# An output projection in 2x2 blocks with seven products, and a feed-forward begun by six chunks on half the tokens

## The chip, the core and the metric

The kernel runs on one core of one Trainium2 chip. The metric is the device time of one execution in microseconds (us), lower being better. TensorE (PE in the profile) multiplies matrices, VectorE (DVE), ScalarE (ACT) and GpSimd (POOL) work elementwise, and SyncE (SP) starts most transfers. Transfers that SP starts run on one queue of DMA engines, those that POOL starts on another. A line such as L158 is line 158 of the kernel profiled.

## The reference

One layer of a decoder on 512 tokens of width 1024, in float32: a feed-forward, token mixing (a recurrent branch and a sliding-window attention side by side, merged by two sigmoid gates and projected by `w_out`), and a second feed-forward, each between two normalisations with learned gains. Cut to the part around the change:

```python
    merged = jax.nn.sigmoid(g_lru) * (y_lru @ w_proj_lru) + jax.nn.sigmoid(g_attn) * (y_attn @ w_proj_attn)
    return merged @ w_out
...
        h = h + rms_norm(m, mix_post_g[l])
        f = swiglu(rms_norm(h, ffn2_pre_g[l]), ffn2_w_gu[l], ffn2_w_down[l])
        h = h + MACARON_SCALE * rms_norm(f, ffn2_post_g[l])
```

## The kernel before

**Products.** Every large product is three matmuls (`mm3`, L157 to L160): each float32 operand is split in a rounded high part and a low part, and high by high, high by low and low by high are summed in PSUM. A weight tile of 128x1024 comes by a transfer on SP's queue (`wload`, L102), ACT rounds it (L112), and DVE subtracts to get the low part (L120). `wget` prepares two tiles ahead.

**Seven products for eight.** Most of both feed-forwards already runs with seven products of blocks in place of eight (`paired`, tiles `f2X`, `f2Y`, `f2Q`). The sums of weight blocks for their second matrix are made in DRAM: SP copies a block (L393), and POOL starts a transfer that accumulates another one onto it (L395).

**The mixer.** Eight gate chunks (`gate_chunk`, L1024) run beside the first heads of the attention. The rotary queries are combined on POOL (L936, L937; tiles `q0m`, `q1m`), stored to DRAM (`q_halves`, L960) and loaded back in another layout (`qt`, L965, four transfers) before the scores (L981, tiles `at00b`, `at10b`, ...). The softmax ends with a multiplication on POOL (L998), and transposes on PE follow (L1004). A loop over eight chunks (L1108 to L1117) then makes the second gated projection and the merged features: `mgh` (ACT, times 0.5, L1115) and `mgl` (DVE, L1116).

**The output projection.** `token_out` (L449) multiplies eight chunks of features by the eight weight tiles of `w_out`, for four tiles of 128 tokens and two halves of the columns: 64 blocks (tiles `woo`), 192 matmuls of 128x512. With `TAILS = 7` the last seven chunks are taken tile by tile, so the first tile of tokens is complete after 0.34 of the work. Behind each tile runs its `epilogue` from `boundary` (L482): squares (L502), an inverse root on POOL (L203), gain and residual (L506, L529), squares again (L534), a spill of the residual to DRAM (L537), the next gain (L542), and then `to_features` (L212): eight transposes on PE (tiles `b2ntp`), a cast to the high part (`u3h`, L222, ACT), the low part (`u3l`, L223, DVE) and a raw copy (`u3r`, L227, ACT), from which `moving` (L694) later makes the operands for `paired`.

**The start of the second feed-forward.** `first_four` (L238) takes four weight chunks with the first half of the tokens (tiles `f2f`, matmuls of 128x256), and then with the second half, so that it can start when two tiles of tokens are there. Four further chunks (tiles `f2g`) take all tokens at once.

**Order.** Except in a few stretches marked `manual_schedule`, a planner sets the order of each engine's instructions: it simulates the program and places each instruction by its own times. Each engine runs its list in order.

Of the kernel before, what the change touches and what calls it, by code (L numbers as in the profile page):

```python
# [42 lines left out]
def hybrid_block_kernel(ctx, tc, x, xt, g1, w_first, gains, gu1, gs1, dn1, w_x, w_gate, w_q, w_k, w_v, w_gl, w_ga, w_pl, w_pa,  # L43
# [70 lines left out]

    def wsplit(upto):
        while len(wready) < min(upto, wcap[0]):
            n = len(wready)
            wround(n + 1)
            w = whi[n]
            V.tensor_tensor(out=w[:, 1, :], in0=raws[n], in1=w[:, 0, :].bitcast(F32),  # L120
                            op=ALU.subtract)
# [3 lines left out]
    def wget():  # L125
        i = wpos[0]
        wpos[0] += 1
        wsplit(i + 1 + AHEAD)
        return wready[i]

# [107 lines left out]
    def first_four(u, name, done):  # L238
# [14 lines left out]
    def gate_up(u, name, first, fast, then, rs=None):  # L253
        ps = []
# [25 lines left out]

        first(u, f"{name}f", done)
        run = paired(fast, name, slot, then(ps))
        for j in range(2, JSTD[name]):
            if j == JSTD[name] - 1:
                next(run)
            bb = []
# [12 lines left out]
    def paired(fast, name, slot, then):  # L299
# [79 lines left out]
        for k in range(3):  # L379
            load(k)  # L380
        sums(0)
        parts(0, 1)
# [65 lines left out]

    def token_out(chunk, n, finish, name, tail_n):  # L449
        half, epilogue, _ = finish  # L450
        banks = {}

        def block(t, c, w, i):
            ph, pl = chunks[c]
            ts_ = slice(t * P, (t + 1) * P)
            if (t, i) not in banks:
                banks[t, i] = bank(f"{name}o{t}{i}")
            ns = slice(i * 512, (i + 1) * 512)
            mm3(banks[t, i], ph[:, c % 4, ts_], pl[:, c % 4, ts_], w[0][:, ns], w[1][:, ns], c == 0, c == n - 1)

        chunks = {}
        tail = []
        for c in range(n):
            w = wget()
            chunks[c] = chunk(c)
            if c < n - tail_n:
                for t in range(NT):
                    for i in range(2):
                        block(t, c, w, i)
                tick()  # L470
            else:
                tail.append((c, w))
        for t in range(NT):
            for i in range(2):
                for c, w in tail:
                    block(t, c, w, i)
            for i in range(2):
                half(t, i, banks[t, i])
            start(epilogue(t))
            tick()  # L480

    def boundary(src, dst, g_post, g_pre, u, scale, name, raw=None, then=None):  # L482
        rhs = []
# [10 lines left out]

        def half(t, i, z, sign=1.0, o=None):
            if t not in sq:
                sq[t], parts[t] = sm(f"{name}ps{t}", 2), [None, None]
# [4 lines left out]
            A.activation(t4(f"{name}sq{t}{i}")[:, :512], z, AF.Square, scale=1.0 / 32.0, accum_out=sq[t][:, i:i + 1])  # L502
            parts[t][i] = o

            def gain():
                V.scalar_tensor_tensor(out=o, in0=z, scalar=sign * scale, in1=g_post[:, cols[i]], op0=ALU.mult,  # L506
                                       op1=ALU.mult)

            if i == 0:
                gain()  # L510
            else:
                late[t] = gain

# [5 lines left out]
        def epilogue(t):  # L519
# [3 lines left out]
            r = inverse(sq[t], f"p{t}")  # L523
            late[t]()
            yield
# [247 lines left out]

    def first_unscaled(u, name, done):
        bs = [bank(f"{name}{i}") for i in range(4)]
# [316 lines left out]
    for c in range(KD):  # L1092
# [12 lines left out]
    while live:  # L1105
        tick()
    mg = []
    for c in range(KD):  # L1108
        s, b = sig_gate(c, ya, "ga")
        if c % 4 == 0:  # L1110
            mg.append((b8(f"mgh{c}", [P, 4, T], F32R), b8(f"mgl{c}", [P, 4, T], F32R)))
        V.scalar_tensor_tensor(out=s, in0=s, scalar=1.0, in1=b, op0=ALU.add, op1=ALU.mult)
        V.tensor_tensor(out=s, in0=s, in1=m1[c // 4][:, c % 4, :], op=ALU.add)
# [6 lines left out]
    u3 = new_u("u3")  # L1120
    hs2 = [dram.tile([P, D], F32, name=f"h2_spill{t}") for t in range(NT)]
    raw3 = [b8(f"u3r{i}", [P, 4, T]) for i in range(2)]
    mv3 = {}
    finish = boundary(hs, hs2, g_post, g_pre, u3, 1.0, "b2", raw3, lambda: moving(raw3, "u3", mv3))
    for _ in range(2):
        finish[2]()
# [11 lines left out]
def _layout(inputs):  # L1138
# [47 lines left out]
    a["w_pa"] = chunks(wa)  # L1186
    a["w_o"] = c(f["w_out"].reshape(KD, P, D))
    a["gu2"], a["gs2"] = gu(f["ffn2_w_gu"])[:JSTD["f2"]], pairs_of(f["ffn2_w_gu"], JSTD["f2"])
# [40 lines left out]
```

## Time and profile before

| what | value |
|---|---|
| median of 3 runs | 1119.62 us (1118.8 to 1120.09) |
| the profiled execution | 1119.82 us |
| its span | 1118.0 us |
| PE busy | 1103.2 us, 6558 matmuls |
| DVE busy | 895.0 us |
| ACT busy | 591.8 us |
| POOL busy | 78.0 us |
| first matmul of the output projection | 728.90 us |
| first matmul of the paired stage of the second feed-forward | 823.03 us |

The span is the profiled stretch from its first to its last instruction; the 1.82 us between it and the time of the same execution lie around it. In a timeline a row gives the start, the length, the engine, the line and the tiles, and in brackets how long the engine stood idle before and what released it. Matmuls overlap in the pipeline, so a matmul's cost is the distance between starts rather than its length.

### The profile page before, as it was taken

To read this page: it belongs to the slowest core of one execution; us is meant where nothing else is said; L and a number is where in the kernel's file an instruction comes from. 1 tells how busy PE (TensorE), PEld (TensorE's weight loads), DVE (VectorE), ACT (ScalarE), POOL (GpSimd) and SP (SyncE) were. 2 spreads that over 40 slices of the span, in tenths; PEclk is the share of its full clock that TensorE was granted. 3 is DMA by queue.
4 is the path that set the end of the run, shared out by engine and by line. 5 is a ranking of instruction groups with operands and counts; after the bars stand their busy time and mean duration, and the time that the engine had idled before them with its cause. 6 is when DMAs were issued, how large, how long until landed. Compare 5 with 4: busy or idle time off the path is not lost.

```text
span 1118.0 us, 16771 instructions
## 1 busy us (share of the span) xinstructions
PE 1103.2 (99%) x6558; PEld 982.3 (88%) x6558; DVE 895.0 (80%) x1277; ACT 591.8 (53%) x991; POOL 78.0 (7%) x82
## 2 busy tenths in 40 slices
PE   9999999999999999999999999999999999999997
PEld 7889999988878888788888888888999999998885
DVE  6998898889998788999777462546859888988895
ACT  7445555465664757576555351436435455556561
POOL 1000000000000101123112000001000000000000
PEclk9999999999999999999999999999999999999999
DMA  9239999664677173622812340523348999455473
GB/s 364 77 125 256 314 280 299 196 226 130 222 266 260 55 207 113 170 57 76 263 58 95 113 169 19 207 95 132 113 122 255 299 274 310 117 173 192 146 269 115
DMA packets 53280, 202.07 MB, mean 181 GB/s; under 512 B 6353, under 2 KB 6481, under 8 KB 48465
## 3 DMA queue, kind: packets, MB, share of 16 engines
q1 hardware_dynamic: 45424, 163.77, 43.3%
q0 software_dynamic: 3456, 23.07, 10.6%
q10 hardware_dynamic: 4320, 14.16, 3.4%
q8 instruction: 51, 0.84, 0.3%
q14 instruction: 29, 0.23, 0.1%
HBM read 189.44 MB, written 57.67 MB: 221 GB/s over the span
## 4 chain that ended last, share of the span: by engine, by line
PE 88%; DVE 8%; issue 1%; DMA 1%; ACT 1%; POOL 0%; SPq 0%; DVEq 0%; POOLq 0%; ACTq 0%
PE f2X L160 5%; PE f2X L159 5%; PE f2X L158 5%; PE f1X L160 4%; PE f1X L158 4%; PE f1X L159 4%; PE f2Q L160 2%; PE f2Q L159 2%; PE f2Q L158 2%; PE f1Q L159 2%; PE f1Q L158 2%; PE f1Q L160 2%; DVE w L120 2%; PE f1f L790 2%; PE glg L158 1%
## 5 line engine op out<-in xcount | busy, mean ns | idle before, releaser
L120 DVE TENSOR_TENSOR w<-wraw,w 128x1024 fp32r<-128x1024 f32 x168 | 197.5, 1196 | 29.4 <-ACT w L112 27.9
L112 ACT CAST w<-wraw 128x1024 fp32r<-128x1024 f32 x168 | 163.3, 1011 | 24.3 <-PE glp L160 7.3
L160 PE MATMUL f1X<-u1m,f1W 128*128 128x256 f32 x256 | 72.5, 283 | 0.1
L159 PE MATMUL f1X<-u1m,f1W 128*128 128x256 f32 x256 | 72.4, 283 | 0.0
L158 PE MATMUL f1X<-u1m,f1W 128*128 128x256 f32 x256 | 72.4, 283 | 0.0
L160 PEld LDWEIGHTS f1X<-u1m,f1W 128*128 128x128 f32 x256 | 49.1, 192 | 0.3 <-DVE f1W L329 0.3
L159 PEld LDWEIGHTS f1X<-u1m,f1W 128*128 128x128 f32 x256 | 49.1, 192 | 0.1
L158 PEld LDWEIGHTS f1X<-u1m,f1W 128*128 128x128 f32 x256 | 49.1, 192 | 0.1
L160 PE MATMUL f2X<-u3m,f2W 128*128 128x256 f32 x144 | 40.9, 284 | 0.1
L160 PE MATMUL f2X<-u3h,f2W 128*128 128x256 f32 x144 | 40.8, 283 | 0.0
L158 PE MATMUL f2X<-u3m,f2W 128*128 128x256 f32 x144 | 40.8, 283 | 0.0
L158 PE MATMUL f2Q<-u3m,f2W 128*128 128x256 f32 x144 | 40.8, 283 | 0.0
L159 PE MATMUL f2Q<-u3m,f2W 128*128 128x256 f32 x144 | 40.8, 283 | 0.0
L160 PE MATMUL f2Q<-u3m,f2W 128*128 128x256 f32 x144 | 40.8, 283 | 0.0
L159 PE MATMUL f2X<-u3l,f2W 128*128 128x256 f32 x144 | 40.8, 283 | 0.0
L159 PE MATMUL f2X<-u3m,f2W 128*128 128x256 f32 x144 | 40.7, 283 | 0.0
L158 PE MATMUL f2X<-u3h,f2W 128*128 128x256 f32 x144 | 40.7, 283 | 0.0
L158 PE MATMUL f1Q<-u1m,f1W 128*128 128x256 f32 x128 | 36.2, 283 | 0.0
L159 PE MATMUL f1Q<-u1m,f1W 128*128 128x256 f32 x128 | 36.2, 283 | 0.0
L160 PE MATMUL f1Q<-u1m,f1W 128*128 128x256 f32 x128 | 36.2, 283 | 0.0
L159 PE MATMUL f1X<-w,f1y 128*128 128x512 f32 x88 | 34.5, 392 | 0.4 <-DVE w L120 0.4
L159 PE MATMUL f2X<-w,f2y 128*128 128x512 f32 x88 | 34.5, 392 | 0.4 <-DVE w L120 0.4
(845 smaller groups left out, 3750.3 us busy)
## 6 DMA issues: line engine op xcount, KB each, us to landing
wraw<-wsum SPq DMA_DIRECT2D x40, 512.0 KB, 4.3
wsum<-in_dn_dram SPq DMA_DIRECT2D x16, 1024.0 KB, 9.6
wraw<-in_dn_dram SPq DMA_DIRECT2D x30, 512.0 KB, 5.0
f2L<-in_gs_dram SPq DMA_DIRECT2D x18, 512.0 KB, 5.0
f2R<-in_gs_dram SPq DMA_DIRECT2D x18, 512.0 KB, 4.9
wraw<-in_gu_dram SPq DMA_DIRECT2D x16, 512.0 KB, 5.9
f1L<-in_gs_dram SPq DMA_DIRECT2D x16, 512.0 KB, 5.5
f1R<-in_gs_dram SPq DMA_DIRECT2D x16, 512.0 KB, 5.7
```

The lines of the kernel that those rows point to most:

```text
L112: A.copy(w[:, 0, :], raws[n])
L120: V.tensor_tensor(out=w[:, 1, :], in0=raws[n], in1=w[:, 0, :].bitcast(F32), op=ALU.subtract)
L158: PE.matmul(o, lhsT=ah, rhs=bh, start=start, stop=False, skip_group_check=reopen)
L159: PE.matmul(o, lhsT=ah, rhs=bl, start=False, stop=False, skip_group_check=reopen)
L160: PE.matmul(o, lhsT=al, rhs=bh, start=False, stop=stop, skip_group_check=reopen)
L790: PE.matmul(bs[i], lhsT=lw[:, i * P:(i + 1) * P], rhs=rx, start=k == 0 and n == 0, stop=k == KD - 1 and n == 2)
```

## The change

The output projection becomes a product of 2x2 blocks by a scheme with seven block products. The merged features are cut in two halves of features and two of tokens, `w_out` in two halves of rows and two of columns. Seven products (in the order 1, 2, 6, 5, 3, 7, 4), each with four chunks of features and two tiles of tokens, give 56 blocks and 168 matmuls of 128x512, summed in three pairs of PSUM banks (`woX`, `woY`, `woQ`). Between them ACT copies banks out (`snap`: `woa`, `wou`, `woq`), and DVE adds (`plus`).

Sums of feature blocks (`os`) are made on DVE and split in high and low parts (`oy`; ACT and DVE, 128x1024 each); the split of `mgh` and `mgl` chunk by chunk is gone, and its factor 0.5 goes into the boundary's scales (`unit`). Four sums of weight blocks are made in DRAM in the tensor `osums`: four copies of 1 MB on SP in the gate chunks 0, 2, 4 and 6, and four accumulating transfers on POOL, which the code starts in the loop after.

`first_six` takes six chunks on half the tokens where `first_four` took four, so two chunks less run with all tokens. Output projection and start of the feed-forward are written in an order by hand, in which the low parts of two weight tiles (`w126`, `w128`) go to POOL. The delays after which `to_features` follows the epilogue (`FEATURE_LAG`) change.

```diff
--- before.py
+++ after.py
...
-TAILS = 7
...
-FEATURE_LAG = {"b1": (7, 9, 7, 3), "b2": (3, 3, 3, 3)}
+FEATURE_LAG = {"b1": (7, 9, 7, 3), "b2": (1, 1, 5, 6)}
...
+    osums = dram.tile([P, 4, 4 * 512], F32, name="osums")
+    osum = [osums[:, i, :] for i in range(4)]
...
-            worder += [w_o[c] for c in range(8)]
+            t1, t2_, t3, t4_ = osum
+            for w in (w_o[0], w_o[1], t2_, t1, w_o[3], t3, t4_):
+                worder += [w[:, i:i + 1024] for i in (0, 1024)]
...
+    def wnow():
+        i = wpos[0]
+        wpos[0] += 1
+        wsplit(i + 1)
         return wready[i]
...
+    def first_six(u, name, done, early):
+        first = []
+        for i in range(6):
+            first.append((wnow(), bank(f"{name}{i}")))
+            if i < 5:
+                wsplit(wpos[0] + 1)
+            feat_chunk(first[i][1], first[i][0], u, HALVES[0])
+            tick()
+        for i, (w, b) in enumerate(first):
+            if i == 2:
+                early()
+            if i >= 4:
+                wsplit(wpos[0] + i - 3)
+            feat_chunk(b, w, u, HALVES[1])
+            tick()
+            done(i, b)
...
-    def token_out(chunk, n, finish, name, tail_n):
...
-            if i == 0:
+            if wait:
+                late[t].append(gain)
+            else:
                 gain()
-            else:
-                late[t] = gain
...
+    oplan = ((0, 2, 0), (2, 3, 2), (1, 3, None), (3, 1, None))
     for c in range(KD):
         gate_chunk(c)
+        if c % 2 == 0:
+            o, a, _ = oplan[c // 2]
+            with tc.issue_after(wdma[wpos[0]].ins):
+                SP.dma_start(osum[o], w_o[a])
...
+        if c % 2 == 0:
+            o, _, b = oplan[c // 2]
+            G.dma_start(osum[o], osum[c // 2 - 2] if b is None else w_o[b], accum_op=ALU.add)
         next_attend()
...
+    def oop_split(i, z, sign=1.0, ks=slice(0, 4)):
+        o = oop[i] if i in oop else oop_new(i)
+        if sign == 1.0:
+            A.copy(o[:, 0, ks], z[:, ks])
+            V.tensor_tensor(out=o[:, 1, ks], in0=z[:, ks], in1=o[:, 0, ks].bitcast(F32), op=ALU.subtract)
...
+    def osum_tile(name, a, b, f, o=None):
+        if o is None:
+            o = t4(name).rearrange("p (k t) -> p k t", k=4)
+        V.tensor_tensor(out=o, in0=a, in1=b, op=f)
+        return o
...
-        mh, ml = mg[-1]
-        A.mul(mh[:, c % 4, :], s, 0.5)
-        V.scalar_tensor_tensor(out=ml[:, c % 4, :], in0=s, scalar=0.5, in1=mh[:, c % 4, :].bitcast(F32),
-                               op0=ALU.mult, op1=ALU.subtract)
+        V.tensor_tensor(out=mg[c // 4][:, c % 4, :], in0=s, in1=m1[c // 4][:, c % 4, :], op=ALU.add)
+        if c == 4:
+            oop_split(1, a11)
+        if c == 5:
+            oop_split(7, osum_tile("os3", a11, a21, ALU.subtract))
+            oop_split(2, a12, ks=slice(0, 2))
...
-    token_out(lambda c: mg[c // 4], KD, finish, "wo", TAILS)
+    def token_out():
+        X, Y, Q = ([bank(f"wo{z}{t}") for t in range(2)] for z in "XYQ")
+        dst = {1: X, 2: Y, 6: X, 5: Q, 3: Q, 7: X, 4: X}
...
+        def unit(i, k, w, tiles):
+            y, n = oop[i], k % 2 * 512
+            for t in tiles:
+                ts_ = slice(t * P, (t + 1) * P)
+                mm3(dst[i][t], y[:, 0, k, ts_], y[:, 1, k, ts_], w[0][:, n:n + 512], w[1][:, n:n + 512],
+                    k == 0 and i in (1, 2, 5), k == 3, True)
...
+        def snap(key, z):
+            sn[key] = [t2(f"wo{key}{t}") for t in range(2)]
+            for t in range(2):
+                A.copy(sn[key][t], z[t])
+
+        def plus(key, z, t):
+            V.tensor_tensor(out=sn[key][t], in0=z[t], in1=sn[key][t], op=ALU.add)
...
+        product(1, first_sums, next_sum)
+        snap("a", X)
...
+        product(2, lambda: oop_split(6, S[2], -1.0), lambda: osum_tile("os4", S[2], a12, ALU.subtract, S[2]))
...
+        product(6, lambda: oop_split(5, S[1]), lambda: oop_split(3, S[2]))
+        snap("u", X)
+        product(5, halves, lambda: oop_split(4, a22))
+        snap("q", Q)
+        product(3, lambda: None, lambda: wsplit(wpos[0] + 4))
+        for t in range(2):
+            plus("u", Q, t)
+            half(t, 1, sn["u"][t], -1.0)
...
+        w = [wnow() for _ in range(2)]
+        for t in range(2):
+            for k in range(4):
+                unit(7, k, w[k // 2], (t,))
+            plus("q", X, t)
+            half(2 + t, 1, sn["q"][t], -1.0, sn["q"][t], True)
...
+        for k in range(4):
+            unit(4, k, w[k // 2], (0,))
+        half(2, 0, X[0])
+        for n in range(2):
+            for k in (2 * n, 2 * n + 1):
+                unit(4, k, w[n], (1,))
+            next(e[n], None)
+        half(3, 0, X[1])
+        wsplit(wpos[0] + 2)
+        next(e[2])
+        next(e[3])
+        wsplit(wpos[0] + 3, G)
+        next(e[2])
+        next(e[3])
+        wsplit(wpos[0] + 4)
+        next(e[2])
+        next(e[3])
+        wsplit(wpos[0] + 5, G)
+        for t in (2, 3):
+            live.append([e[t], next(e[t])])
 
     dn_run = []
-    gate_up(u3, "f2", first_four, lambda: (gs2, blocks(u3, mv3)), begin(dn_run, "f2"))
+    with tc.manual_schedule():
+        token_out()
+        gate_up(u3, "f2", first_six, lambda: (gs2, blocks(u3, mv3)), begin(dn_run, "f2"), j0=3)
```

**POOL around the queries.** The program's order on POOL, before and then changed, from the combination of the first queries to the first softmax:

```order
L937 TENSOR_TENSOR q0m2_4510<-q0m2_4510,q0m1_4509 128x512
L936 TENSOR_TENSOR q0m0_4508<-q0m0_4508,q0m3_4511 128x512
L937 TENSOR_TENSOR q1m2_4596<-q1m2_4596,q1m1_4595 128x512
L936 TENSOR_TENSOR q1m0_4594<-q1m0_4594,q1m3_4597 128x512
L998 TENSOR_TENSOR at00s_4739<-at00s_4739,at00ss_4758 128x512
```

```order
L1111 DMA osums_75<-in_w_o_dram 128x2048 x2
L1111 DMA osums_75<-osums_75 128x2048
L942 TENSOR_TENSOR q0m2_4511<-q0m2_4511,q0m1_4510 128x512
L941 TENSOR_TENSOR q0m0_4509<-q0m0_4509,q0m3_4512 128x512
L942 TENSOR_TENSOR q1m2_4597<-q1m2_4597,q1m1_4596 128x512
L941 TENSOR_TENSOR q1m0_4595<-q1m0_4595,q1m3_4598 128x512
L1111 DMA osums_75<-osums_75 128x2048
L1003 TENSOR_TENSOR at00s_4742<-at00s_4742,at00ss_4761 128x512
```

The planner moved all four accumulating transfers from the later loop to here: three stand ahead of the first queries, the fourth directly behind the second ones. On SP the fourth copy to `osums` stands between a weight load and the first four `qt` loads:

```order
L965 DMA q_halves0_4556<-q0st_4519 128x2048
L105 DMA wraw73_4704<-in_w_gate_dram 128x1024
L1085 DMA osums_75<-in_w_o_dram 128x2048
L970 DMA qt0_4590<-q_halves0_4556 32x4x512 x4
L965 DMA q_halves1_4653<-q1st_4605 128x2048
L105 DMA wraw74_4773<-in_w_q_dram 128x1024
L970 DMA qt1_4696<-q_halves1_4653 32x4x512 x4
```

Before, the same rows stood there without the copy.

**PE at the end of the projection.** The changed order from the middle of the last product's second tile (`woX1`) to the feed-forward's first matmuls:

```order
L169 MATMUL woX1_6986<-w122_7194,oy4_7153 128x512
L227 MATMUL b2ntp00_7329<-ident_135,b2un0_7261 128x128 x4
L227 MATMUL b2ntp01_7336<-ident_135,b2un0_7261 128x128 x4
L167 MATMUL woX1_6986<-w123_7199,oy4_7153 128x512
L168 MATMUL woX1_6986<-w123_7199,oy4_7153 128x512
...
L169 MATMUL woX1_6986<-w123_7199,oy4_7153 128x512
L227 MATMUL b2ntp10_7351<-ident_135,b2un1_7268 128x128 x4
L227 MATMUL b2ntp11_7358<-ident_135,b2un1_7268 128x128 x4
L167 MATMUL f2f0_7423<-u3h0_7226,w124_7222 128x256
L168 MATMUL f2f0_7423<-u3l0_7228,w124_7222 128x256
```

Before, tile 0's transposes stood ahead of the 42 matmuls that the last tile of tokens took; now 6 matmuls of 128x512 lie between tile 0's and tile 1's. In both, the feed-forward follows tile 1's directly. The transposes of tiles 2 and 3, which before stood behind the first matmul of the feed-forward and behind its second chunk, now follow the fifth and the sixth chunk, the latter with the second half of the first chunk directly behind:

```order
L169 MATMUL f2f5_7567<-u3h1_7227,w129_7524 128x256
L227 MATMUL b2ntp30_7592<-ident_135,b2un3_7397 128x128 x4
L227 MATMUL b2ntp31_7599<-ident_135,b2un3_7397 128x128 x4
L167 MATMUL f2f0_7423<-u3h0_7226,w124_7222 128x256
L168 MATMUL f2f0_7423<-u3l0_7228,w124_7222 128x256
```

**DVE and ACT at the same place.** DVE's changed order from the last weight tiles of the projection to the low parts of the first features:

```order
L123 TENSOR_TENSOR w123_7199<-wraw123_7175,w123_7199 128x1024
L1188 TENSOR_TENSOR wou0_7119<-woQ0_6989,wou0_7119 128x512
...
L534 SCALAR_TENSOR_TENSOR b2rh1_7037<-b2rh1_7037,b2p1r_7241 128x512 x2
L1188 TENSOR_TENSOR woq1_7169<-woX1_6986,woq1_7169 128x512
...
L123 TENSOR_TENSOR w124_7222<-wraw124_7192,w124_7222 128x1024
L547 SCALAR_TENSOR_TENSOR b2un0_7261<-b2rh0_7035,b2n0r_7292,g_b2_6976 128x512 x2
L547 SCALAR_TENSOR_TENSOR b2un1_7268<-b2rh1_7037,b2n1r_7296,g_b2_6976 128x512 x2
L232 TENSOR_TENSOR u3l0_7228<-b2ntp00_7329,u3h0_7226 128x4x128
```

The epilogues of tiles 0 and 1 now run together, behind all weight tiles of the projection, where before they ran one after another between its tiles of tokens. On ACT the copies of product 5's banks stand behind two casts of 128x1024:

```order
L506 ACTIVATE b2sq10_7133,b2ps1_7132<-woa1_7032 128x512
L115 CAST w119_7148<-wraw119_7082 128x1024
L1132 CAST oy4_7153<-mg1_6452 128x1024
L1185 COPY woq0_7168<-woQ0_6989 128x512
L1185 COPY woq1_7169<-woQ1_6990 128x512
```

Product 3 adds into the same banks `woQ` and follows product 5 directly on PE.

More of the change, by code (lines that the diff above doesn't have):

```diff
@@ L113, in wround, with wsplit @@
             whi.append(w)
-    def wsplit(upto):
+    def wsplit(upto, eng=V):
         while len(wready) < min(upto, wcap[0]):
@@ L119, in wsplit @@
             w = whi[n]
-            V.tensor_tensor(out=w[:, 1, :], in0=raws[n], in1=w[:, 0, :].bitcast(F32),
+            eng.tensor_tensor(out=w[:, 1, :], in0=raws[n], in1=w[:, 0, :].bitcast(F32),
                             op=ALU.subtract)
@@ L128, in wget @@
         wsplit(i + 1 + AHEAD)
+        return wready[i]
+    def wnow():
+        i = wpos[0]
+        wpos[0] += 1
+        wsplit(i + 1)
         return wready[i]
@@ L251, in split_chunk, with gate_up @@
         V.tensor_tensor(out=pl[:, i, :], in0=p[:, i, :], in1=ph[:, i, :].bitcast(F32), op=ALU.subtract)
-    def gate_up(u, name, first, fast, then, rs=None):
+    def gate_up(u, name, first, fast, then, rs=None, j0=2):
         ps = []
@@ L279, in done, with early @@
                 tail(i // 2, bs[i - 1], b)
-        first(u, f"{name}f", done)
         run = paired(fast, name, slot, then(ps))
-        for j in range(2, JSTD[name]):
+        loads = []
+        def early():
+            if not loads:
+                loads.append(next(run))
+        first(u, f"{name}f", done, early)
+        for j in range(j0, JSTD[name]):
             if j == JSTD[name] - 1:
+                early()
                 next(run)
@@ L380, in paired @@
             load(k)
+        yield
         sums(0)
@@ L447, in paired, with boundary @@
             finish(n - 1)
-    def token_out(chunk, n, finish, name, tail_n):
[L450 to L470, printed above, removed]
-            else:
[L472 to L482, printed above, removed]
+    def boundary(src, dst, g_post, g_pre, u, scale, name, raw=None, then=None, unit=1.0):
         rhs = []
@@ L493, in boundary, with half @@
         sq, parts, late = {}, {}, {}
-        def half(t, i, z, sign=1.0, o=None):
+        def half(t, i, z, sign=1.0, o=None, wait=False):
             if t not in sq:
-                sq[t], parts[t] = sm(f"{name}ps{t}", 2), [None, None]
+                sq[t], parts[t], late[t] = sm(f"{name}ps{t}", 2), [None, None], []
+                wait = wait or i == 1
+            else:
+                wait = True
             if o is None:
@@ L501, in half @@
                 o = rhs[t][:, 1, cols[i]]
-            A.activation(t4(f"{name}sq{t}{i}")[:, :512], z, AF.Square, scale=1.0 / 32.0, accum_out=sq[t][:, i:i + 1])
+            A.activation(t4(f"{name}sq{t}{i}")[:, :512], z, AF.Square, scale=unit / 32.0, accum_out=sq[t][:, i:i + 1])
             parts[t][i] = o
             def gain():
-                V.scalar_tensor_tensor(out=o, in0=z, scalar=sign * scale, in1=g_post[:, cols[i]], op0=ALU.mult,
-                                       op1=ALU.mult)
-            if i == 0:
+                V.scalar_tensor_tensor(out=o, in0=z, scalar=sign * scale * unit, in1=g_post[:, cols[i]],
+                                       op0=ALU.mult, op1=ALU.mult)
+            if wait:
+                late[t].append(gain)
+            else:
                 gain()
-            else:
-                late[t] = gain
         def inverse(ms, z):
@@ L523, in epilogue @@
             r = inverse(sq[t], f"p{t}")
-            late[t]()
+            for gain in late[t]:
+                gain()
             yield
@@ L772, in scaled, with first_unscaled @@
         block(3, 1, hi_)
-    def first_unscaled(u, name, done):
+    def first_unscaled(u, name, done, early):
         bs = [bank(f"{name}{i}") for i in range(4)]
@@ L1106, in hybrid_block_kernel, with oop_new @@
         tick()
-    mg = []
+    mg = [b8(f"mg{i}", [P, 4, T]) for i in range(2)]
+    lo_, hi_ = slice(0, 256), slice(256, 512)
+    a11, a21, a12, a22 = (mg[i][:, :, tok] for i in range(2) for tok in (lo_, hi_))
+    oop = {}
+    def oop_new(i):
+        oop[i] = b8(f"oy{i}", [P, 2, 4, 256], F32R)
+        return oop[i]
+    def oop_split(i, z, sign=1.0, ks=slice(0, 4)):
[3 more added lines that the diff above has]
+            V.tensor_tensor(out=o[:, 1, ks], in0=z[:, ks], in1=o[:, 0, ks].bitcast(F32), op=ALU.subtract)
+        else:
+            A.activation(o[:, 0, ks], z[:, ks], AF.Copy, scale=sign)
+            V.scalar_tensor_tensor(out=o[:, 1, ks], in0=z[:, ks], scalar=sign, in1=o[:, 0, ks].bitcast(F32),
+                                   op0=ALU.mult, op1=ALU.subtract)
@@ L1108, in hybrid_block_kernel @@
+    def osum_tile(name, a, b, f, o=None):
[3 more added lines that the diff above has]
+        return o
     for c in range(KD):
         s, b = sig_gate(c, ya, "ga")
-        if c % 4 == 0:
-            mg.append((b8(f"mgh{c}", [P, 4, T], F32R), b8(f"mgl{c}", [P, 4, T], F32R)))
         V.scalar_tensor_tensor(out=s, in0=s, scalar=1.0, in1=b, op0=ALU.add, op1=ALU.mult)
-        V.tensor_tensor(out=s, in0=s, in1=m1[c // 4][:, c % 4, :], op=ALU.add)
@@ L1186, in _layout @@
     a["w_pa"] = chunks(wa)
-    a["w_o"] = c(f["w_out"].reshape(KD, P, D))
+    w = f["w_out"].reshape(2, 4, P, 2, 512)
+    a["w_o"] = c(np.stack([w[j, :, :, i].transpose(1, 0, 2).reshape(P, 2048) for i in range(2) for j in range(2)]))
     a["gu2"], a["gs2"] = gu(f["ffn2_w_gu"])[:JSTD["f2"]], pairs_of(f["ffn2_w_gu"], JSTD["f2"])
```

47 lines of the change are left out of this document (41 added, 6 removed).

## The prediction

> **What bounds the kernel now.** I read the page's first block first, then the list of what PE waited for, then busy time by stretch, and timelines where a stretch was not full.
>
> ```profile
> span 1118.0 us, 16771 instructions
> PE 1103.2 (99%) x6558; PEld 982.3 (88%) x6558; DVE 895.0 (80%) x1277; ACT 591.8 (53%) x991; POOL 78.0 (7%) x82
> ...
> 446.00:514.00 68.00, 66.12 (x329) 55.34 (x328) 65.69 (x111) 40.82 (x96) 12.59 (x7) 1.00 0.39 107
> 728.90:772.90 44.00, 44.00 (x200) 36.52 (x199) 21.28 (x35) 14.89 (x35) 3.30 (x6) 1.00 0.23 83
> 772.90:806.00 33.10, 31.35 (x240) 29.98 (x239) 31.80 (x40) 20.99 (x32) 1.09 (x2) 1.00 0.45 144
> ...
> PE f2f L158 <- ACT u3h L222: 1.2, 1, 1.2
> PE at02t L1004 <- POOL at02s L998: 1.2, 1, 1.2
> PE at10b L981 <- DMA qt<-q_halves: 1.1, 1, 1.1
> ```
>
> PE is busy 1103.2 of 1118.0 us, so a matmul less is time less wherever PE waits for nothing, and a new wait is time more. The stretches (their columns: length, then busy time of PE, weight load, DVE, ACT, POOL) are the attention's start, the output projection, and the feed-forward's start. In the projection PE is full, and DVE is busy for only 21.28 of 44.00 us. At the attention's start DVE works 65.69 of 68.00 us and cannot take a delay. Two waits lie at each end of the change: for the first features, and for a `qt` load and the softmax behind it.
>
> **The products.** PE's timeline gives the price of a matmul as the distance of starts:
>
> ```profile
> 761.99 0.39 PE L160 MATMUL woo<-w,mgl 128*128 128x512 f32 x1
> 762.22 0.39 PE L158 MATMUL woo<-w,mgh 128*128 128x512 f32 x1
> 762.45 0.39 PE L159 MATMUL woo<-w,mgh 128*128 128x512 f32 x1
> 762.67 0.39 PE L160 MATMUL woo<-w,mgl 128*128 128x512 f32 x1
> ...
> 773.09 0.40 PE L160 MATMUL woo<-w,mgl 128*128 128x512 f32 x1
> 773.32 1.03 PE L218 MATMUL b2ntp<-ident,b2un 128*128 128x128 f32 x8
> 775.60 0.39 PE L158 MATMUL f2f<-u3h,w 128*128 128x256 f32 x1 [1.24 <-ACT u3h L222]
> 775.82 1.04 PE L218 MATMUL b2ntp<-ident,b2un 128*128 128x128 f32 x8
> 776.62 0.36 PE L158 MATMUL f2f<-u3h,w 128*128 128x256 f32 x1
> 777.49 0.39 PE L159 MATMUL f2f<-u3l,w 128*128 128x256 f32 x1 [0.51 <-DVE u3l L223]
> ...
> 779.03 0.28 PE L159 MATMUL f2f<-u3l,w 128*128 128x256 f32 x1
> 779.15 0.28 PE L160 MATMUL f2f<-u3h,w 128*128 128x256 f32 x1
> ```
>
> Three starts in 0.68 us make 0.227 us for 128x512; 168 for 192 matmuls save 24 x 0.227 = **5.44**. A 128x256 matmul takes 0.12, more than half: two more chunks in halves turn 48 x 0.227 = 10.88 into 96 x 0.12 = 11.52, **+0.64**. The transposes are the same in number.
>
> The old waits at the feed-forward's start go, since everything around them is rewritten. Eight transposes take 0.9 (775.82 to 776.62, with a hand-over), so from 773.32 the first `f2f` was due at 774.22 and came at 775.60: 1.38. The second gap, 776.62 to 777.49 for a matmul of 0.12, is 0.75. Together **-2.13**.
>
> **The new waits in the stage.** I lay the changed order on durations of these groups (lines, engine, shapes, count, then busy time and mean, then idle time before):
>
> ```profile
> L120 DVE TENSOR_TENSOR w<-wraw,w 128x1024 fp32r<-128x1024 f32 x30 | 35.2, 1221 | 8.4 <-ACT w L112 8.4
> L112 ACT CAST w<-wraw 128x1024 fp32r<-128x1024 f32 x30 | 29.9, 1047 | 8.5 <-issue 6.4 <-PE gag L159 1.3 <-PE gag L160 0.7
> L506 DVE SCALAR_TENSOR_TENSOR b2rh<-woo,g_b 128x512 f32<-128x512 f32 x8 | 5.5, 683 | 6.0 <-ACT b2sq L502 6.0
> L223 DVE TENSOR_TENSOR u3l<-b2ntp,u3h 128x512 fp32r<-128x512 f32 x8 | 5.2, 684 | 0.4 <-ACT u3h L222 0.4
> L227 ACT COPY u3r<-b2ntp 128x512 f32<-128x512 f32 x8 | 4.7, 584 | 1.3 <-DVE u3l L223 0.9 <-DVE b2un L542 0.3
> L222 ACT CAST u3h<-b2ntp 128x512 fp32r<-128x512 f32 x8 | 4.3, 592 | 2.0 <-PE b2ntp L218 2.0
> ...
> L998 POOL TENSOR_TENSOR at11s<-at11s,at11ss 128x1024 f32<-128x1024 f32 x1 | 2.8, 2833 | 10.5 <-DVE at11ss L997 10.5
> L998 POOL TENSOR_TENSOR at03s<-at03s,at03ss 128x1024 f32<-128x1024 f32 x1 | 1.9, 1895 | 2.1 <-DVE at03ss L997 2.1
> ```
>
> (a) Product 3 adds into the banks that ACT copies out after product 5. The first copy takes 0.58, can start when the last matmul of its bank is through, and only the 0.68 of the other tile's matmuls lies beside it, pipeline and hand-over included: **+0.5**, from 0.1 (copy at once) to 0.6; behind it on ACT wait the casts of the next weights.
>
> (b) From the projection's start to the end of product 3 DVE has 18 steps of 128x1024 at 1.17 (35.2 by 30) and 7 of 128x512 at 0.69: 25.9, and some 2 of hand-overs from ACT, while PE has 5 products of 24 x 0.227 and the wait of (a): 27.7. The cover that DVE had in this stage is gone. Call S the end of product 3 on PE; DVE reaches the first addition there at about S+0.6. Its order then gives two additions and two gains to S+3.6, the addition for tile 2 to 4.2, four residual steps to 6.8, another addition to 7.4, two small steps that wait for ACT's squares to 8.65, a weight's low part to 9.85, tile 0's gain to 11.15 and tile 1's to 12.4. PE wants tile 0's after products 7 and 4 but 6 matmuls, S+9.5: 1.65 late. After 8 transposes, 6 matmuls, 8 transposes PE is at S+14.3. Tile 1's cast stands on ACT behind two raw copies of tile 0, which wait for its low parts (13.0 and 13.7): cast 14.9, low part 15.5. That is 1.05 more, together **+2.7**. If DVE's hand-overs hide behind its queue, 1.4; if ACT, whose list is as long, adds a cast, 3.5.
>
> (c) The low part of the third chunk's weight goes to POOL, behind the inverse root of tile 3, which this order reaches at about S+19.3. POOL took 1.89 to 2.83 for 128x1024; with 2.3 and a hand-over it ends at 21.8, and PE, two half chunks of 2.88 after 15.4, wants it at 21.05: **+0.75**, from 0 to 1.7. Behind it on POOL wait the roots of tiles 2 and 3, wanted some 5 us later. The second such weight comes after them: 0 to 0.7, taken as 0.
>
> The Trainium skill ("GPSIMD Engine Reference", section 2.1 Instruction dispatch) gives POOL a floor of about 2.5 cycles per element for two inputs; at the page's 1.2 GHz my estimate is 2.13 us for 1024. This trace does not agree that it is a floor, with 1.895; by the page's figure the wait would be 0.6.
>
> (d) Tile 3's transposes stand directly before a matmul that needs their cast. Half the transposes cover 0.45 of cast (0.59) and low part (0.68), with hand-overs: **+0.95**, from 0.5 to 1.5. The old start, 2.13 with a busy ACT, is the nearest row. Later operands have the remaining half chunks as cover: five of them, 14.4 us, before the next thing that uses all tokens.
>
> The stage's new waits come to 4.9.
>
> **The weight sums.** Four 1 MB copies on SP and four accumulating transfers move ahead of or between the queries. Here are SP's own rows, then transfers from issue to landing with an accumulation under way (843.4 to 847.0) and without (854.6), then the packets of 846 to 850, and two more transfers:
>
> ```profile
> 446.11 1.75 SPq L965 DMA_DIRECT2D qt<-q_halves  x4
> 456.66 0.34 SPq L960 DMA_DIRECT2D q_halves<-q1st  x1
> 460.94 1.74 SPq L965 DMA_DIRECT2D qt<-q_halves  x4
> ...
> 457.39 0.89 PE L981 MATMUL at00b<-kp,qt 128*128 128x128 f32 x7
> ...
> 451.04 2.21 POOL L936 TENSOR_TENSOR q1m<-q1m,q1m 128x512 f32<-128x512 f32 x1
> ...
> wsum<-in_dn_dram POOLq DMA_DIRECT2D x1, 1024.0 KB, 10.0
> f2L<-in_gs_dram SPq DMA_DIRECT2D x1, 512.0 KB, 9.2
> ...
> f2L<-in_gs_dram SPq DMA_DIRECT2D x1, 512.0 KB, 4.3
> ...
> q0 software_dynamic: 91, 0.75, 91.7%
> q1 hardware_dynamic: 28, 0.11, 7.8%
> ...
> qt<-q_halves SPq DMA_DIRECT2D x16, 256.0 KB, 6.1
> ...
> q_halves<-q1st SPq DMA_DIRECT2D x1, 1024.0 KB, 4.3
> ```
>
> An accumulation (q0) lets SP's queue (q1) through with 28 packets of 119: a load that follows it by 1.4 us takes 9.2 in place of 4.3. The fourth accumulation stands behind `q1m`, which ended at 453.25, and would run to about 463; the store of the second queries is issued at 456.66, half-way. I take it 2.5 late, from 0 (the accumulation starts after the store) to 4.9. The `qt` loads behind it shift by as much, and PE already waits for them. Of the 2.5, PE gets back the 1.2 of its later wait for POOL at most, and DVE's 2.3 idle us in 68 give 0.3 more: **+1.0**. The earlier three stand ahead of `q0m`, and the fourth copy ahead of the first `qt`. Those loads, the last issued at 447.5, land by 453.6 (6.1 after), and PE wants them at 457.39: 3.8 in hand. The copy is 1 MB like the store, which landed in 4.3, and holds the queue for less than that: I take 0, and up to 1.3 if `q0m` is late as well.
>
> **Sum.** -5.44 + 0.64 - 2.13 + 4.9 + 1.0 = -1.03. The profiled execution took 1119.82, 0.2 over the median of the runs; from the median 1119.62 it is 1118.6.
>
> **The rivals.** *The waits are no larger than before.* If DVE is 1.5 quicker through the products than by my count, (b) falls to its lower end or below, (c) and (d) to theirs, 2.1 in all, and the fourth accumulation misses the store: -5.44 + 0.64 = -4.8, 1114.8. For it: in the old stage DVE stood at 21.28 of 44.00 us and hand-overs were mostly hidden. Against it: the new order gives DVE nearly the whole of PE's time.
>
> *The accumulations hold the queries.* On POOL three of them wait for SP's copies with `q0m` queued behind. If the third copy lands some 3 us after 436 and the fourth accumulation covers the whole store (+4.9), PE loses 5 to 6 at the first scores, gets 1.2 back, and with the stage at 6 the sum is -5.44 + 0.64 - 2.13 + 6.0 + 4.3 = +3.4, 1123.0. It decides from 4.3 on upstream with my stage, as then the gain of 2.03 turns into a loss of 2.27. For it: DVE at 65.69 of 68.00; against: 3 us of slack.
>
> *The queues share evenly.* If SP's store got as many packets as the accumulation, it would be late by about its own remaining half, 1.3, which the 1.2 and 0.3 swallow: sum -2.03, 1117.6. The rows speak against it, 28 packets to 91. The Trainium skill ("DMA: Bandwidth & Descriptors", Queues, rings and completion order) has each engine take turns between queues packet by packet. That rule would give this rival; the trace does not agree, by those packets.
>
> That the change does less than it says I leave out: PE's order has the 168 matmuls.
>
> **How the numbers follow.** Forecast 0.42, from 1116.9 to 1120.6; waits no larger 0.30; queries held 0.21; even sharing 0.07. About 0.2%, 2.24 us, is what a measurement of this kernel can tell from no change. The forecast gives 0.10 to faster and 0.32 to same; the second case 0.29 and 0.01; the third 0.20 slower and 0.01; even sharing 0.03 and 0.04: faster 0.42, same 0.38, slower 0.20. The range of 8 in 10 reaches to the second case and most of the third: 1114.6 to 1122.4.
>
> **What would show it.** Right: PE's waits name DVE's gain of tile 0 at the transposes, 1 to 2 us, ACT's cast at the first `f2f`, about 1, POOL at the third chunk, and the wait of `at10b` for `qt` grows to 3 to 4. Wrong: those waits under 0.5 each (then the first rival), or `at00b` waiting for `qt`, with `q0m` later than 438 (then the second); DVE idle in the projection for over 5 us would show my queue too long.

## The result and the profile after

The changed kernel takes 1126.25 us (median of 4 runs, 1125.59 to 1126.98) where the kernel before, beside it, takes 1119.86: 1.0058 of its time, with a 95% interval from 1.0046 to 1.0070. It is 6.4 us slower. The forecast was 1118.6, with a range up to 1122.4. The page and the list of what PE waited for, of the changed kernel:

```profile
span 1123.6 us, 16868 instructions
PE 1103.9 (98%) x6582; PEld 982.5 (87%) x6582; DVE 913.6 (81%) x1291; ACT 602.5 (54%) x1003; POOL 87.6 (8%) x88
```

```profile
PE at10b L986 <- DMA qt<-q_halves: 4.0, 1, 4.0
...
PE at00b L986 <- DMA qt<-q_halves: 1.4, 1, 1.4
PE at02t L1009 <- POOL at02s L1003: 1.2, 1, 1.2
PE f2f L169 <- POOL w L123: 1.1, 2, 0.7
PE f2f L167 <- ACT u3h L231: 1.0, 2, 0.7
PE f2f L168 <- DVE u3l L232: 0.7, 2, 0.3
PE f2f L169 <- DVE w L123: 0.5, 1, 0.5
```

The span grew by 5.6 us, and the waits alone don't make it: at the queries they grew by 1.4 + 2.9, and at the feed-forward's start by 1.6 (3.3 for 1.7), while the products should have saved 4.8. Two rows of PE's timeline say where the time went:

```profile
736.75 0.39 PE L167 MATMUL woX<-w,oy 128*128 128x512 f32 x1
...
829.75 0.28 PE L167 MATMUL f2X<-u3h,f2W 128*128 128x256 f32 x1
```

The projection starts at 736.75 where it started at 728.90: **7.85 us are lost ahead of it**, in a part of the program whose list on PE is unchanged. From there to the first paired product it is 93.00 us against 94.13: the rewritten stage itself **gains 1.13**. (The rest of the difference in the spans is the last store, which landed 2.0 us after its issue here and 3.0 before.) What is missing beside the waits shows in busy time by stretch, whose third column from the right is the clock granted to PE:

```profile
460.00:462.00 2.00, 2.00 (x7) 1.56 (x7) 1.27 (x3) 1.12 (x2) 0.00 (x0) 0.54 1.20 164
462.00:464.00 2.00, 2.00 (x7) 1.58 (x6) 2.00 (x4) 1.45 (x2) 0.00 (x0) 0.60 0.65 143
...
476.00:478.00 2.00, 1.66 (x10) 1.60 (x11) 0.99 (x3) 0.46 (x3) 0.00 (x0) 0.81 0.84 336
478.00:480.00 2.00, 2.00 (x6) 1.54 (x6) 2.00 (x8) 1.71 (x8) 0.00 (x0) 0.50 0.00 0
480.00:482.00 2.00, 2.00 (x9) 1.65 (x8) 1.78 (x4) 0.47 (x2) 1.04 (x1) 0.84 0.00 0
```

The figures in brackets are counts of instructions. PE counts as fully busy from 460 to 464 and from 478 to 480, but gets only 6 or 7 matmuls through in 2 us, where 10 or 11 are usual. Behind each of the two waits its clock is at one half for about 3.5 us. Taking 2 us times what the clock lacks, the first stretch costs 0.92 + 0.80 = 1.7 and the second 0.38 + 1.00 + 0.32 = 1.7. So the loss ahead of the projection is 1.39 and 2.87 of waiting and 3.4 of slow clock, 7.7 of 7.85.

Why `qt` came late is in the timelines of POOL and SP, and in the packets of 458 to 463 (q0 is POOL's queue, q1 SP's):

```profile
438.27 0.81 POOL L1111 DMA_DIRECT2D osums<-osums  x1 [14.56 <-DMA osums<-in_w_o_dram]
438.83 1.58 POOL L942 TENSOR_TENSOR q0m<-q0m,q0m 128x512 f32<-128x512 f32 x1
...
455.24 0.81 POOL L1111 DMA_DIRECT2D osums<-osums  x1
```

```profile
446.69 0.50 SPq L1085 DMA_DIRECT2D osums<-in_w_o_dram  x1
448.76 2.13 SPq L970 DMA_DIRECT2D qt<-q_halves  x4
458.70 0.34 SPq L965 DMA_DIRECT2D q_halves<-q1st  x1
...
468.49 1.74 SPq L970 DMA_DIRECT2D qt<-q_halves  x4
```

```profile
q0 software_dynamic: 103, 0.84, 104.0%
...
q_halves<-q1st SPq DMA_DIRECT2D x1, 1024.0 KB, 9.8
```

The third accumulation waited on POOL for SP's copy until 438.27 and held `q0m` behind it: 438.83 for 436.17. The fourth copy went ahead of the first `qt` loads. The fourth accumulation, issued at 455.24, was under way when the second store was issued at 458.70. From 458 to 463 it had 103 packets, and that view has no row for q1 at all: SP's queue, with the store on it, moved nothing. The store landed 9.8 us after its issue in place of 4.3. The second `qt` loads were issued at 468.49, 7.5 us later than before.

### The profile page after: what moved, and what is told of

Same layout as the page of the kernel before. It is cut to its first block, busy times and chain, and to the rows that moved or that the text cites. A ratio compares the mean times of both kernels' runs of the same rounds, so it can differ in the third digit from the quotient of the medians.

```text
span 1123.6 us, 16868 instructions
## 1 busy us (share of the span) xinstructions
PE 1103.9 (98%) x6582; PEld 982.5 (87%) x6582; DVE 913.6 (81%) x1291; ACT 602.5 (54%) x1003; POOL 87.6 (8%) x88
## 5 line engine op out<-in xcount | busy, mean ns | idle before, releaser
L123 DVE TENSOR_TENSOR w<-wraw,w 128x1024 fp32r<-128x1024 f32 (+1 forms) x172 | 202.3, 1194 | 25.9 <-ACT w L115 24.2
L115 ACT CAST w<-wraw 128x1024 fp32r<-128x1024 f32 x174 | 169.2, 1012 | 27.0 <-PE glp L169 7.4
L1147 DVE SCALAR_TENSOR_TENSOR gas<-gas,gap 128x512 f32<-128x512 f32 x8 | 5.5, 688 | 45.2 <-PE gap L169 45.2
```

What stands on the lines that cost most here:

```text
L115: A.copy(w[:, 0, :], raws[n])
L123: eng.tensor_tensor(out=w[:, 1, :], in0=raws[n], in1=w[:, 0, :].bitcast(F32), op=ALU.subtract)
```

## Experiments

The theory at this point: the transfers of the weight sums make the queries late, PE waits, and each wait is followed by a stretch at half clock. Rivals: the order of DVE and ACT that the planner changed with them makes the waits; the slow clock has some other cause; only some of the transfers matter. All times stand against runs of the kernel before on the same chip (1119.9 in the first and third group, 1120.4 in the second).

### The sums made elsewhere

The copies and accumulations move to the loop over the second gated projection. The list of PE up to the projection stays row for row that of before.

```diff
-        if c % 2 == 0:                      # in the gate chunks
-            ...SP.dma_start(osum[o], w_o[a])
-        if c % 2 == 0:                      # in the loop behind
-            ...G.dma_start(osum[o], ..., accum_op=ALU.add)
     for c in range(KD):
         s, b = sig_gate(c, ya, "ga")
+        if c in (0, 1, 2, 3):
+            o, a, z = oplan[c]
+            with tc.issue_after(wdma[wpos[0]].ins):
+                SP.dma_start(osum[o], w_o[a])
+            tc.keep_in_program_order(G.dma_start(osum[o], osum[c - 2] if z is None else w_o[z], accum_op=ALU.add))
```

> The changed kernel with its four weight-sum copies and four accumulations moved from the gate chunks to the loop over the second gated projection, some 200 us later, where POOL has nothing to do; PE's order up to the output projection is row for row that of before. Theory (transfers on the queues make qt late, each of the two waits of PE is followed by some 3.5 us at half clock): the 7.8 us that the changed kernel has lost at the first matmul of the projection go, both waits back to before's (at00b none, at10b 1.1), no window at a clock under 1.0 there, 1118.4 us. Rival 1 (DVE's and ACT's changed order upstream makes the waits): no change, 1126. Rival 2 (the low clock has another cause than the waits): 3.2 of the 7.8 stay, 1121.6.

Measured: 1117.16 us, 0.9975 of before (0.9965 to 0.9984). At the queries PE waits as it did before the change:

```profile
PE at02t L1009 <- POOL at02s L1003: 1.2, 1, 1.2
PE at10b L986 <- DMA qt<-q_halves: 1.1, 1, 1.1
```

The clock stays at 1.00 from 452 to 496, and the projection starts at 728.13. 9.1 us are back. That is 1.2 under the theory's 1118.4. In the profiles 0.8 against before lies in the program's first 8 us, where the kernels do not differ: one and the same matmul of the first stage starts at 6.33 here and at 7.15 before.

The second rival falls: the half clock went with the waits. The first does not fall by the time alone, since DVE and ACT run here in the order of before up to the loop over the second gated projection, so the order went back together with the transfers. The changed kernel's trace settles it. Its rows leave that order at these two, and at none before them:

```profile
464.03 0.63 ACT L1038 ACTIVATE gp<-gp 128x512 f32<-128x512 f32 x1
...
465.30 0.68 DVE L1039 SCALAR_TENSOR_TENSOR gp<-gp,gt 128x512 f32<-128x512 f32 x1
```

Both lie behind the first wait, which ended at 459.07, and behind the issue of the second store at 458.70, after which `qt` waited for transfers alone. So the changed order came after the delay and did not make it.

### Which transfers

The first of two kernels moves only the fourth copy and the fourth accumulation to the later loop; the other moves all four accumulations and leaves the copies.

```diff
-        if c % 2 == 0:
+        if c in (0, 2, 4):                  # copies and accumulations 1 to 3 stay; the fourth pair in the later loop
```

> As the changed kernel, but only the fourth copy and the fourth accumulation are moved to the later loop; the first three stay ahead of q0m. Theory (the fourth pair does it, the copy on SP's queue ahead of the first qt loads and the accumulation during the second store): at00b does not wait, at10b waits 1 to 2, 1118.5 to 1120. Rival (the first three hold q0m and with it the first queries): at00b still waits 1 or more with a stretch at half clock behind it, 1121 to 1122.5.

Measured: 1119.29 us (ratio 0.9998, 0.9988 to 1.0007). PE does not wait at `at00b`:

```profile
PE gt L169 <- DVE w L123: 1.4, 1, 1.4
...
PE at10b L986 <- issue: 0.8, 1, 0.8
```

So the fourth pair costs 1126.25 - 1119.29 = 7.0. The first three are not free either: against the kernel with all sums moved they cost 2.1, but through another door. They hold `q0m` (437.71 for 435.38 there), as the rival had it, but it reached PE through DVE's queue and not through `qt`: DVE's step behind `q0m` moved from 438.85 to 441.02, the rows after it by as much, and one low part came 1.4 late.

```profile
441.02 0.68 DVE L947 TENSOR_TENSOR q0st<-q0m,q0st 128x512 fp32r<-128x512 f32 x1
```

That wait of 1.4 did not halve the clock; it is 1.00 in every stretch behind it.

```diff
     for c in range(KD):
         s, b = sig_gate(c, ya, "ga")
+        if c < 4:                           # the four copies stay in the gate chunks
+            o, _, z = oplan[c]
+            tc.keep_in_program_order(G.dma_start(osum[o], ..., accum_op=ALU.add))
```

> As the changed kernel, with its four copies where they are and the four accumulations in the later loop. Theory (the accumulations shut SP's queue out; the copies only add their own bytes): the second store lands 4.3 to 5 after its issue, at10b waits 1 to 2, at00b under 0.5, 1118.5 to 1119.5. Rival (the copies on SP's own queue do it): at00b waits 1 or more and at10b 3 or more, 1122 to 1126.

Measured: 1118.09 us (0.9990, 0.9981 to 1.0000), a little under the theory's window. The second store, and PE's wait for the loads behind it:

```profile
q_halves<-q1st SPq DMA_DIRECT2D x1, 1024.0 KB, 4.6
```

```profile
PE at10b L986 <- DMA qt<-q_halves: 0.3, 1, 0.3
```

The wait is below the theory's 1 to 2 as well. The accumulations cost 1126.25 - 1118.09 = 8.2. For the copies 1118.09 - 1117.16 = 0.9 is left, but in the two profiles that difference is there ahead of any copy (the same matmul of the first stage starts at 7.58 and 6.33), so no price of the copies is shown.

### The sums alone

The kernel before, with the same eight transfers put in the same places. Their result is not used, and the projection is that of before.

> The kernel before, with the four copies and four accumulations of the changed kernel added at the same places and their result not used. Theory: it loses what the changed kernel loses upstream, 7.8 us (waits 1.4 and 4.0 in place of 0 and 1.1, and two stretches of 3.5 us at half clock): 1127.5. Rival (the sums cost only together with the new order of DVE and ACT): under 1122.

Measured: 1127.93 us, 1.0075 of before (1.0060 to 1.0090): the sums alone cost 8.1 us, the theory's 7.8 and a little more. Waits, then busy time and clock behind the longer one:

```profile
PE at10b L981 <- DMA qt<-q_halves: 5.5, 1, 5.5
...
PE at00b L981 <- DMA qt<-q_halves: 1.0, 1, 1.0
```

```profile
476.00:480.00 4.00, 4.00 (x14) 3.52 (x15) 2.89 (x10) 2.17 (x9) 0.00 (x0) 0.50 0.29 114
480.00:484.00 4.00, 4.00 (x17) 3.28 (x16) 2.57 (x6) 2.37 (x10) 1.04 (x1) 0.86 0.00 0
```

Here the first wait was 1.0 and the clock behind it stayed at 1.00; only the second was followed by the half clock, from 476 to about 481. The price splits differently, 1.0 + 4.4 of waiting and one longer slow stretch of some 2.4, for nearly the same sum.

### A wait without any transfer

To separate the clock from the queues, one wait is put into the projection of the best kernel at that time (low_early, below): ahead of the second product PE runs one matmul on a tile that ACT makes by one, three or six copies of the first product's result. The second product overwrites what it wrote.

```diff
         snap("a", X)
+        z = t2("pause", F32R)
+        for i in range(1):                  # 3, 6
+            A.copy(z, sn["a"][1] if i == 0 else z.bitcast(F32))
+        PE.matmul(Y[0], lhsT=z[:, :P], rhs=z, start=True, stop=True)
```

> low_early with one wait put into the projection, with no transfer in it: ahead of the second product PE runs one matmul on a tile that ACT makes from the first product's result by one further copy, about 1.8 us of waiting. Theory (a wait of PE itself halves its clock for some 3.5 us once it is long enough; 1.2 us did not, 1.4 with its hand-overs did in the changed kernel): at the edge, 1117 without and 1118.7 with a stretch at half clock. Rival (the half clock belongs to the crowded queues): never under 1.00 here, 1117.

> As pause1 with three copies, about 2.9 us of waiting. Theory: a stretch of 3 to 4 us at half clock behind it, which costs 1.6 to 1.8 more than the wait: 1115 + 2.9 + 1.7 = 1119.6, with some 0.5 for the casts held up on ACT. Rival: 1118.

> As pause1 with six copies, about 4.6 us of waiting. Theory: the same one stretch at half clock, no longer than after the shorter wait: 1115 + 4.6 + 1.7 = 1121.3 and up to 1 for the casts held up on ACT. Rival: 1119.6 to 1120.6 with the clock at 1.00.

Measured: 1116.56, 1120.13 and 1122.12 us, where the kernel without a wait took 1114.95 in another group, whose kernel before was 0.6 slower. Each one's wait, and its busy time and clock behind it, in this order:

```profile
PE woY L1206 <- ACT pause L1205: 1.3, 1, 1.3
...
737.00:739.00 2.00, 2.00 (x10) 1.62 (x10) 1.96 (x2) 2.00 (x4) 0.00 (x0) 1.00 0.86 289
```

```profile
PE woY L1206 <- ACT pause L1205: 2.6, 1, 2.6
...
737.00:739.00 2.00, 1.92 (x5) 1.54 (x6) 0.56 (x1) 1.66 (x3) 0.00 (x0) 0.54 0.77 217
739.00:741.00 2.00, 2.00 (x7) 1.57 (x6) 2.00 (x3) 2.00 (x3) 0.00 (x0) 0.60 0.95 336
```

```profile
PE woY L1206 <- ACT pause L1205: 4.6, 1, 4.6
...
741.00:743.00 2.00, 2.00 (x6) 1.62 (x5) 2.00 (x2) 2.00 (x3) 0.00 (x0) 0.50 0.92 373
743.00:745.00 2.00, 2.00 (x8) 1.59 (x8) 2.00 (x3) 2.00 (x3) 0.00 (x0) 0.79 0.83 258
```

Because of the two groups the price is better read inside the traces. From the projection's start to the first paired product they take 92.46, 95.31 and 97.70 us, where low_early takes 90.57. So the wait of 1.3 cost 1.9 and left the clock alone. That of 2.6 cost 4.7, and that of 4.6 cost 7.1, each with one stretch at half clock: 2.1 and 2.5 us more than was waited, of which the clock is about 1.7 to 2 and the extra matmul 0.3. The half clock belongs to the wait, wherever it comes from.

How long a wait has to be is not shown. All four waits of 2.6 or more were followed by the half clock (2.6, 4.0, 4.6 and 5.5), and none up to 1.3 was. Between them the length alone does not decide: 1.4 was enough in the changed kernel, but 1.4 in fourth_late, 1.6 in the kernel with six copies and 1.7 in first_order (below) were not.

```profile
PE at10b L992 <- DMA qt<-q_halves: 1.7, 1, 1.7
...
470.00:472.00 2.00, 2.00 (x14) 1.78 (x14) 2.00 (x7) 1.96 (x7) 0.00 (x0) 1.00 0.10 41
```

The Trainium skill ("TensorE: Matmul & The Clock Gate", section What's actually happening) has PE fall back to half rate after an idle window of about 3.4 us, and recover after as long a time of work. The stretches of 3.5 us in the changed kernel agree with the recovery; that of sums_only was nearer 5. The fall came after waits of 2.6, and in one profile 1.4, so as a limit on idle time the 3.4 does not hold in these runs.

### The stage itself

The trace of the changed kernel shows something at the two low parts on POOL. DVE's and POOL's rows, from two timelines:

```profile
783.27 2.80 DVE L534 SCALAR_TENSOR_TENSOR b2rh<-b2rh,b2p2r 128x512 f32<-128x512 f32 x1
...
790.05 3.54 DVE L547 SCALAR_TENSOR_TENSOR b2un<-b2rh,b2n2r,g_b 128x512 f32<-128x512 f32 x2 [0.61 <-POOL b2n2r L212]
```

```profile
783.13 2.38 POOL L123 TENSOR_TENSOR w<-wraw,w 128x1024 fp32r<-128x1024 f32 x1
...
790.50 2.54 POOL L123 TENSOR_TENSOR w<-wraw,w 128x1024 fp32r<-128x1024 f32 x1
```

A residual step that takes 0.74 elsewhere took 2.80, and a pair of gains 3.54 for 1.4, each just while POOL worked. Starting from the kernel with the sums moved, the next ones put these low parts on DVE: at the same places, then ahead.

```diff
-        wsplit(wpos[0] + 3, G)
+        wsplit(wpos[0] + 3)
...
-        wsplit(wpos[0] + 5, G)
+        wsplit(wpos[0] + 5)
```

> sums_late with the low parts of the third and fifth chunk's weights (w126, w128) on DVE in place of POOL, at the same places of the order. Theory (POOL's subtraction of two operands stops DVE's own two-operand steps while it runs, as the residual step of 2.80 us and the gain pair of 3.54 us beside it suggest): those steps take 0.7 and 1.4, PE's waits for w126 and w127 (0.56 and 0.70) go, but w128 now stands behind four gains on DVE and comes 1 to 2.4 late in place of 0.87; together 1116.2 to 1117.5. Rival (the long steps waited for their own inputs): they stay long, DVE is later by two subtractions, 1118 to 1119.

Measured: 1115.96 us, 0.9959 of before (0.9943 to 0.9974).

```profile
776.83 0.75 DVE L534 SCALAR_TENSOR_TENSOR b2rh<-b2rh,b2p2r 128x512 f32<-128x512 f32 x1
...
782.43 1.41 DVE L547 SCALAR_TENSOR_TENSOR b2un<-b2rh,b2n2r,g_b 128x512 f32<-128x512 f32 x2
```

The long steps are gone: POOL's subtraction, 2.4 us, had stopped DVE for 2.1 each time, more than the 1.2 that the same step takes on DVE, so that it relieved DVE of nothing. It also came out better than expected, since the order puts the second low part ahead of the gains, not behind them as I had read it. The Trainium skill ("SBUF — State Buffer", section Who interferes with whom) says that the one thing two engines contend for is the port pair that they share, and that it is held exclusively; these durations agree.

```diff
         next(e[3])
-        wsplit(wpos[0] + 3, G)
+        wround(wpos[0] + 5)
+        wsplit(wpos[0] + 4)
         next(e[2])
         next(e[3])
-        wsplit(wpos[0] + 4)
+        wsplit(wpos[0] + 5)
         next(e[2])
         next(e[3])
-        wsplit(wpos[0] + 5, G)
```

> sums_late with both low parts on DVE and put ahead: w126 and w127 before the residual steps of tiles 2 and 3, w128 before their gains. Theory: the waits of 0.56, 0.70 and 0.87 go, 2.1 in all, and the transposes of tiles 2 and 3 still find their gains done: 1115.0. Rival (DVE is the bound there, whoever does the low parts): the wait moves to the transposes of tile 2, 1116.5 to 1117.5.

Measured: 1114.95 us, 0.9952 (0.9937 to 0.9966). PE no longer waits for any weight there. From the projection's start to the first paired product it takes 90.57 us, where the kernel with the sums moved takes 92.99: 2.4, the theory's 2.1 and a little more.

Three more take the waits at the first features. The first moves w124's low part and tile 0's raw copies; the second takes the transposes of tiles 2 and 3 one chunk earlier as well (`FEATURE_LAG` 1, 1, 4, 5); the third is the first one with w124's low part between the gains of tile 0 and tile 1.

> low_early, with the low part of the first chunk's weight (w124) moved from before the gains of tiles 0 and 1 to behind tile 0's low parts, and tile 0's raw copies on ACT moved behind tile 1's casts. Theory (DVE's queue makes the first transposes late, ACT's copies the first f2f): the first wait at the transposes (0.22 and 0.16) goes, the waits of the first f2f (0.88 and 0.61) fall to about 0.8 together: 1114.2. Rival (ACT's squares and casts ahead set it): as low_early, 1115.0.

> first_order with the transposes of tiles 2 and 3 one chunk earlier, behind the fourth and the fifth chunk, so that a half chunk lies between tile 3's and the matmul that needs its cast. Theory: the wait of 0.99 behind tile 3's transposes goes: 1113.3. Rival (gains of tile 2 or the sixth weight not ready that early): the wait moves to those transposes or to f2f5, 1114 to 1115.

> first_order with the low part of w124 between the gains of tile 0 and tile 1 on DVE, so that tile 1's low parts no longer stand behind it (there the first f2f waited 1.32 between its first two matmuls). Theory: that gap falls to about 0.7, tile 1's transposes come up to 0.2 later: 1114.2. Rival (tile 1's cast on ACT sets the low part anyway): 1114.6.

Measured: 1114.63, 1115.03 and 1114.32 us. The waits of the second, then of the third:

```profile
PE f2f L168 <- DVE u3l L234: 0.9, 1, 0.9
...
PE f2f L169 <- DVE w L123: 0.7, 1, 0.7
PE b2ntp L229 <- DVE b2un L553: 0.5, 1, 0.5
```

```profile
PE f2f L168 <- DVE u3l L234: 0.9, 2, 0.6
```

first_order lies between theory and rival: the wait at the transposes went, but the gap between the first two `f2f` matmuls grew to 1.3, as w124 then stood ahead of tile 1's low parts. lag45 is the rival's: the wait behind tile 3 went to the gain of tile 2 (0.5) and to the sixth weight (0.7). The last one is the fastest of all, **1114.32 us, 0.9944 of before (0.9929 to 0.9959)**, 5.5 us under the kernel before and 11.9 under the changed one; it can't be told from first_order by time (0.3 us).

## Why the prediction was wrong

**The step that failed** is the term for the weight sums, "+1.0". It measured 7.85 at the projection's start, and 8.1 as a part by itself. Four things in it were wrong.

- The store was taken 2.5 late, between 0 and 4.9. It took 9.8 in place of 4.3 and was issued 2.0 later (458.70 for 456.66). The row that I quoted, a load at 9.2 for 4.3, was the right one, and I took half of it.
- The first three accumulations and the fourth copy, "I take 0, and up to 1.3 if `q0m` is late as well". `q0m` was 2.7 late, behind the third accumulation, and the first scores waited 1.4. DVE's step behind `q0m` moved `q1m` from 449.80 to 451.83 too, and with it the second store.
- "PE gets back the 1.2 of its later wait for POOL at most": it got back nothing. The wait at `at02t` is 1.1 or 1.2 in every kernel of this study, whatever happened ahead: what it waits for is shifted with PE.
- The slow clock, 3.4 of the 7.85, was not in the sum, and in no rival. The row that could have told was not in the profile of before: no wait in that stage was over 1.2 us there, and its clock was 1.00. The prediction asked only how long PE would wait, not at what rate it goes on.

The second rival named the mechanism and the place (accumulations ahead of `q0m` and across the store, the first scores waiting), and its sign came: `at00b` waited for `qt`, and `q0m` started at 438.83, later than 438. It put 4.3 on it, 1123.0 in all. With the clock's 3.4 it would have been at 1126.4. That this meets the measured time is in part luck: its 4.3 is 5 to 6 less 1.2 that did not come back, its 6.0 for the stage measured 5.3, and the shorter last store was in no sum. The first rival falls with the waits, 5.3 in the stage where it had 2.1, and even sharing with the packets, 103 of POOL's queue to none of SP's.

**The products and the old waits** came as worked out: the stage holds 168 matmuls at 0.227 and 288 at 0.12.

**The new waits in the stage** were 4.9 by the sum and 5.3 by the starts of PE's matmuls, differently spread. (a) 0.27 for 0.5. (b) 1.9 for 2.7: DVE's first addition came 0.6 late as I had it, and the transposes waited only 0.4, since DVE's steps follow each other in 0.6 where I took up to 0.69, but the cast and the low part behind made 1.5 for 1.05. (c) 0.56 for 0.75, and then two that I had put at nothing: w127 on DVE 0.70, w128 on POOL 0.87. Both go once no low part is on POOL (low_early), and the rows say how: POOL stops DVE, a cost of the hand-over to POOL that the step left out. I had priced POOL's own time only (2.4 by the trace, 2.3 taken). The row of 1.895 that I had set against a floor for two inputs multiplies by a tile of 128x4; the subtraction of two full tiles took 2.38 and 2.54. (d) 1.0 for 0.95. The stage as a whole gained 1.13 where the sum gave 2.03; 0.4 of that is these waits, and 0.5 is spread over hand-overs that I could not assign.

**What the change was worth** without its two side effects is seen in the last kernels, each against the kernel before in its group: 2.7 us with the sums moved, 4.5 with the low parts on DVE as well, 5.5 with them put ahead. That this is near the 4.8 of the products alone is in part luck. By the starts of PE's matmuls the stage itself gains 1.1, 3.0 and 3.6. About 1.1 more lies behind the first paired product, where the kernel before takes 295.0 us and every kernel with the change 293.8 to 294.0; the shorter last store is in it, and no run shows its cause.

## What to carry to other kernels

Transfers that are "not urgent" are placed by what they collide with: an accumulating transfer of 1 MB shut the other queue out for some 5 us, and it belongs where no store or load on the way to PE is near. A planner that hoists it will not see that, so pin it. Price a new wait on PE with what follows it: from 2.6 us on, and perhaps from 1.4, add 1.7 to 2.4 for the half clock. And work given to POOL is relief for DVE only if it does not stop DVE while it runs.

## What the runs showed of the hardware that was not expected

- PE's clock fell to one half for about 3.5 to 5 us behind each single wait of 2.6 us or more, with or without transfers, in the middle of a program that is 98% busy. A wait of 1.3 left it alone; of four between 1.4 and 1.7, one was followed by it.
- A two-operand step of POOL on 128x1024 (2.4 to 2.5 us) held a two-operand step of DVE, or a pair of them, for 2.1 us.
- While an accumulating transfer ran, SP's queue got no packet from 458 to 463 though a 1 MB store had been issued on it at 458.70; the store took 9.8 us for 4.3. With the accumulations moved and the plain copies left where they were, it took 4.6.
